# A bank for one values tile, smaller first pieces and fewer warm-up products in a hybrid decoder layer

## The chip, the cores and the metric

The kernel runs on one core of a Trainium2 chip. The metric is the device time of one execution in microseconds. The engines are named as in the profile: PE (TensorE's products) and PEld (its weight loads), DVE (VectorE), ACT (ScalarE), POOL (GpSimd) and SP (SyncE, which here issues DMAs).

## What is computed

One decoder layer on 512 tokens of width 1024, in float32. A normalized input is projected once; three groups of heads use the columns (dilated attention, gated linear attention "GLA", block-sparse attention); then come an output projection and a feed-forward part with a squared ReLU.

```python
h = rmsnorm(x, norm1_w)
proj = h @ w_in
aq, ak, av, bq, bk, bv, br, ba, cq, ck, cv = split(proj)
y_a = dilated_attention(aq, ak, av, bias_a)
y_b = gla(bq, bk, bv, br, ba, w_a2, b_a, gla_norm_w)   # ends with * silu(br)
y_c = moba_attention(cq, ck, cv, bias_c)
x = x + concat(y_a, y_b, y_c) @ w_out
x = x + square(relu(rmsnorm(x, norm2_w) @ w_ff1)) @ w_ff2
return rmsnorm(x, final_norm_w)
```

## The kernel before

**Products in three parts.** PE takes its operands in a rounded 32-bit form. To keep float32 accuracy every operand is cut in a high and a low part (`xh`, `xl` of the activations, `wh`, `wl` of the weights), and each product is made three times (high by high, low by high, high by low). The high part is a copy with a cast, on ACT or DVE; the low part is a subtraction on DVE.

**An order written out by hand.** The kernel's streams are Python generators. A planner (`Plan`, L111) runs them: it keeps a clock for each engine, gives each operation a cost of its own estimate, and places next the operation that can start first by those clocks, the lower priority number first among equals. What it places goes to its engine's queue in that order; the hardware then runs each queue in order, and semaphores that follow from the data hold an instruction until its inputs are there and its output's place is free. Streams also wait for events (`("wait", ...)`, set by `fire`) and for resources (`("take", r)`, given back by `give(r)`); both act on the planner's order. The PSUM banks are such resources: two of kind "mm", two "s", two "pt", one "o" and one "g" (L219).

**The start.** `start` (L1759) issues the DMA of the first weight block `wraw` on ACT's queue, sets `ones`, and gives PE a number of products of `ones` with itself (`WARM`, L28), whose result nobody reads; each shows as two passes in the profile. `first_x` brings the first block of the transposed input in two DMAs into `x0n`: 256 tokens and the norm weights (272 columns), then the other 256. `norm_weights` (L1746) copies 16 columns of norm weights to `nw` on DVE. `scaled_x(0)` makes `xh` of the first block by two activations of 256 columns on ACT, and later `xl` on DVE and squares on ACT. `parts` (L310) makes `wh` of the first weight block by one cast of 528 columns on DVE after `nw`; for all later blocks it uses ACT. `zeros` has POOL clear several tiles, the six `klz` halves among them.

**The first product.** `first` (L673) goes over eight blocks of 128 input columns. For each block and each of the three parts it makes four products of 272 weight columns (`av`, one per tile of 128 tokens) and two of 512 tokens (`bq`, `bk`), into six banks of kinds "s", "o", "g" and "pt".

**The first values product.** `v_proj(0)` (L1091) then makes, for each of the four token tiles, 24 products of 512 columns (`vps`: eight blocks, three parts, a group of three at a time) into a bank of kind "mm". `v_out` (L1073) empties the bank by two activations on ACT, `v` and `rg`, and gives it back. Meanwhile the GLA streams make small products that also take "mm" banks (`dps`, then the transposes `ktp`), and batches of level products (`lp`) into "s" and "pt" banks, which DVE empties by predicated copies into `attn`. `bias_table` (L622) uses "g" for the first half of a table and "o" for the second (`vt`, copied by DVE to `vals`). After `v_proj(0)` come the query and key products (`qkps`), whose weights `parts` cuts with ACT (`wh`) and DVE (`wl`). Almost every instruction carries line 141 in the profile, that of the helper that issues them, so the tiles' names tell them apart.

Of the kernel before, what the change touches and what calls it, by code (L numbers as in the profile page):

```python
# [12 lines left out]
AF = mybir.ActivationFunctionType  # L13
# [11 lines left out]
KBS = ((2,), (1, 3), (0,))  # L25
KO = (0, 1, 3, 4, 2, 5, 6, 7)
TAU = 1.0 / 16.0
LC, LT, LW, LN, WARM = 1.0, 0.5, 1.0, 0.0, 9  # L28
BIGS, SLOTS, WPAIRS, SCRATCH = 43, 22, 5, 2048
NC = 5  # L30
ZL, PL = 4.5, 3.2
# [76 lines left out]
PE, ACT, DVE, POOL, SP = (Engine(n) for n in ("tensor", "scalar", "vector", "gpsimd", "sync"))  # L108


class Plan:  # L111
# [15 lines left out]
    def spawn(self, gen, prio=0):  # L127
        self.streams.append(dict(gen=gen, prio=prio, item=None, at=self.now, sent=None, n=len(self.streams)))

    def fire(self, key, t=None):  # L130
        self.done[key] = self.now if t is None else t

    def give(self, res):
        self.free[res].append(self.now)
# [75 lines left out]
def hybrid_block_kernel(ctx: ExitStack, tc: tile.TileContext, x0_d, xT_d, x_d, w0_d, wv_d, wqk_d, w1_d, w2_d,  # L210
# [10 lines left out]
    spawn, fire, give = plan.spawn, plan.fire, plan.give  # L221
    late = dict(copy=LC, tt=LT)

    def slot(name, dt=F32, shape=(128, 512)):
        return sp.tile(list(shape), dt, name=name, tag="slot", bufs=SLOTS)

    def big(name, dt=F32, shape=(128, 1024)):
        return wp.tile(list(shape), dt, name=name, tag="big", bufs=BIGS)
# [4 lines left out]
    def bank(tag, name):  # L233
        return ps.tile([128, 512], F32, name=name, tag=tag, bufs=BANKS[tag])

    def f32(ap):
        return ap.bitcast(F32)
# [10 lines left out]
    nw = consts.tile([128, 2, KT], F32)  # L248
# [30 lines left out]
    xh, xl = ([t[:, k] for t in [big(n, F32R, (128, 2, 512)) for _ in range(4)] for k in range(2)] for n in ("xh", "xl"))  # L279
# [30 lines left out]
    def parts(key, src, n=1024):  # L310

        yield ("take", "w")
        yield ("take", "big")
        yield ("take", "big")
        hi = big("wh", F32R)
        lo = big("wl", F32R)
        loaded[key] = (hi, lo)
        if key == ("0", 0):
            yield ("wait", "nw")
        yield (DVE.tensor_copy(hi[:, :n], src[:, :n]) if key == ("0", 0) else ACT.activation(hi[:, :n], src[:, :n], AF.Copy))  # L320
        fire(("wh", key))
        if key == ("0", 0):
            yield ("wait", ("xl", 0))
        yield DVE.tensor_tensor(lo[:, :n], src[:, :n], f32(hi[:, :n]), op=OP.subtract)
        fire(("w", key))

    def give_w():
        give("w")
        give("big")
        give("big")  # L330
# [193 lines left out]
    def scaled_x(k):  # L524
        if k == 0:

            halves = (slice(0, 256), x0n[:, :256]), (slice(256, 512), x0n[:, 272:528])
            n_ = x0n[:, 256:257]
            for i, (cs, src) in enumerate(halves):
                yield ("wait", ("x", 0, i))  # L530
                yield ACT.activation(xh[0][:, cs], src, AF.Copy, scale=n_)
                fire(("xh", 0) if i else "xh00")
            yield ("wait", ("wh", ("0", 0)))
            for cs, src in halves:
                yield DVE.scalar_tensor_tensor(xl[0][:, cs], src, n_, f32(xh[0][:, cs]), op0=OP.mult, op1=OP.subtract)
            fire(("xl", 0))
            for cs, src in halves:
                yield ACT.activation(ssx[:, cs], src, AF.Square)
            fire(("ssx", 0))
            give("big")  # L540
            return
        yield ("wait", ("x", k))
        yield ("wait", "nw")
        yield ACT.activation(xh[k], xT[k], AF.Copy, scale=nw[:, 0, k:k + 1])
        fire(("xh", k))
        if k == 1:
            yield ("wait", ("w", ("0", 0)))
        yield DVE.scalar_tensor_tensor(xl[k], xT[k], nw[:, 0, k:k + 1], f32(xh[k]), op0=OP.mult, op1=OP.subtract)
        fire(("xl", k))
        sq = slot("sq")  # L550
        yield ("wait", ("ssx", k - 1))
        yield ACT.activation(sq, xT[k], AF.Square)
        yield DVE.tensor_tensor(ssx, ssx, sq, op=OP.add)
        fire(("ssx", k))
# [118 lines left out]
    def first():  # L673

        for k in range(KT):
            yield ("wait", ("xh", k) if k else "xh00")
            yield ("wait", ("wh", ("0", k)))
            wh, wl = loaded.pop(("0", k))
            for i, (xx, ww) in enumerate(((xh[k], wh), (xl[k], wh), (xh[k], wl))):
                if i:  # L680
                    yield ("wait", (("xl", k), ("w", ("0", k)))[i - 1])
                kw = dict(start=(k == 0 and i == 0), stop=(k == KT - 1 and i == 2))
                ops = ([PE.matmul(acc_v[t][:, :272], xx[:, t * 128:(t + 1) * 128], ww[:, :272], **kw) for t in range(NT)]
                       + [PE.matmul(acc_q, ww[:, 272:400], xx, **kw), PE.matmul(acc_k, ww[:, 400:528], xx, **kw)])
                if k + i == 0:
                    yield ops[:2]
                    yield ("wait", ("xh", 0))
                    ops = ops[2:]
                yield ops
            give_w()  # L690
            if k == 5:
                fire("first6")
        fire("first")
# [376 lines left out]
                             stop=(last and i == len(ks) - 1 and j == 2))  # L1070
                   for j, (ww, xx) in enumerate(((wh, ah[k]), (wh, al[k]), (wl, ah[k])))]

    def v_out(g, t, acc):  # L1073

        n = 512 if g else 256
        v = vS[g, t] = vT[(g, t - t % 2) if g else (0, 0)][:, t % (2 if g else 4)]
        yield ACT.activation(v, acc[:, :n], AF.Copy, scale=rstd[:, t:t + 1])
        fire(("v", g, t))
        if not g:
            sg, rg = (x[:, t % 2] for x in gates[t // 2])  # L1080
            yield ACT.activation(rg, acc[:, n:], AF.Copy, scale=nrstd[:, t:t + 1])
        give("mm")
        if g:
            return
        yield ("prio", 2)
        yield [DVE.tensor_scalar(sg, rg, 80.0, None, op0=OP.min), DVE.tensor_tensor(rg, rg, gw, op=OP.mult)]
        fire(("gate", t))
        if t % 2:
            spawn(gate(t // 2), 2)

    def v_proj(g):  # L1091
        if not gates:
            gates.extend(tuple(slot(x, shape=(128, 2, 256)) for x in ("sg", "rg")) for _ in range(2))
        hl = []
        for c in range(4):
            yield ("wait", ("w", ("v", g, c)))
            hl.append(loaded.pop(("v", g, c)))
        for t in range(NT):
            yield ("take", "mm")
            acc = bank("mm", "vps")  # L1100
            ts = slice(t * 128, (t + 1) * 128)
            for k in range(KT):
                wh, wl = hl[k // 2]
                w_ = slice((k % 2) * 512, (k % 2) * 512 + 512)
                yield [PE.matmul(acc, xx[:, ts], ww[:, w_], start=(k + j == 0), stop=(k == 7 and j == 2))
                       for j, (xx, ww) in enumerate(((xh[k], wh), (xl[k], wh), (xh[k], wl)))]
                if t == NT - 1 and k % 2:
                    give_w()
                if t == NT - 1 and g and k % 2:
                    give("big")  # L1110
                    give("big")
                    if k > 4:
                        give("w")
            if t == 0:
                yield ("wait", "rstd")
                yield ("wait", "consts")
            if t % (2 if g else 4) == 0:
                yield ("take", "big")
                vT[g, t] = big("v", shape=(128, 2, 512) if g else (128, 4, 256))
                if t:  # L1120
                    fire("vT")
            spawn(v_out(g, t, acc), 0.5)

    def q_out(p, acc):
        yield ("wait", "R")
# [52 lines left out]
    def gate(i):  # L1178


        for t in (2 * i, 2 * i + 1):
            yield ("wait", ("gate", t))
        sg, rg = gates[i]
        y, d = (slot(x, shape=(128, 2, 256)) for x in ("y", "d"))
        yield ACT.activation(sg, sg, AF.Exp)
        yield ACT.activation(y, sg, AF.Ln, bias=1.0)
        yield ACT.activation(y, y, AF.Exp, scale=-1.0)
        yield [DVE.scalar_tensor_tensor(d, sg, 1.0, y, op0=OP.add, op1=OP.mult),
               DVE.scalar_tensor_tensor(d, d, -2.0, y, op0=OP.add, op1=OP.mult),
               DVE.tensor_tensor(rg, d, rg, op=OP.mult)]  # L1190
        G.append(rg.rearrange("p t c -> p (t c)"))
        if i:
            fire("G")
# [550 lines left out]
            fire(("x", 0, i))  # L1744

    def norm_weights():  # L1746
        yield ("wait", ("x", 0, 0))
        yield DVE.tensor_copy(nw.rearrange("p a b -> p (a b)"), x0n[:, 256:272])
        fire("nw")

# [133 lines left out]
```

## Time and profile before

| | us |
|---|---|
| median of three runs | 556.94 |
| lowest, highest | 556.84, 557.59 |
| the profiled execution | 556.4 |
| its span, first to last instruction | 554.6 |

Times of instructions are from the span's start. In the lines of the timeline the columns are start, duration, engine, line, operation, out<-in tiles, shape and count, and in brackets the idle time of the engine before it with what ended it. A matmul's end is modelled; the distance from one start to the next says more than its duration. In the tables by engine, (x) is the number of instructions. DMA was busiest at the start; the page's two rows on it in 40 slices of the span are:

```profile
DMA  8930304699998969803679714688815788937504
GB/s 314 392 136 2 110 6 132 215 281 253 273 285 275 316 201 376 171 1 115 152 157 281 212 72 153 152 221 234 228 38 190 160 223 230 212 79 209 106 1 152
```

### The profile page before, as it was taken

What the parts mean: (1) busy time and instruction counts of PE and PEld (TensorE: products, weight loads), DVE (VectorE), ACT (ScalarE), POOL (GpSimd) and SP (SyncE); (2) the same over time, 40 slices, a digit from 0 to 9 for tenths busy, and PEclk for the clock granted to TensorE, in tenths of its full rate; (3) what the DMA queues carried; (4) which work ended last, traced back from release to release, by engine and by line L of the source; (5) the groups of instructions that cost most, each with busy time, mean ns of one, the idle gap of its engine ahead of it and who ended that gap; (6) DMA issues with size and microseconds to landing.
All of it is one profiled execution on the core that took longest, in us unless ns stands there. A gap on an engine that the chain in (4) does not pass through costs nothing.

```text
span 554.6 us, 9438 instructions
## 1 busy us (share of the span) xinstructions
PE 546.1 (98%) x3530; PEld 484.8 (87%) x3530; DVE 488.0 (88%) x793; ACT 351.2 (63%) x588; POOL 84.6 (15%) x135
## 2 busy tenths in 40 slices
PE   9999999999999999999999999999999999999995
PEld 8987888888888888999988999988999888999884
DVE  6969998999987899899899858999589999588986
ACT  7746465668576546768855448864377753479654
POOL 7100000431524001100111100111000111202031
PEclk9999999999999999999999999999999999999998
DMA  8930304699998969803679714688815788937504
GB/s 314 392 136 2 110 6 132 215 281 253 273 285 275 316 201 376 171 1 115 152 157 281 212 72 153 152 221 234 228 38 190 160 223 230 212 79 209 106 1 152
DMA packets 33518, 101.44 MB, mean 183 GB/s; under 512 B 5026, under 2 KB 5712, under 8 KB 33472
## 3 DMA queue, kind: packets, MB, share of 16 engines
q1 hardware_dynamic: 24816, 73.76, 39.3%
q0 software_dynamic: 8368, 26.53, 24.5%
q8 instruction: 28, 0.46, 0.3%
q10 hardware_dynamic: 288, 0.53, 0.3%
q14 instruction: 18, 0.15, 0.1%
HBM read 92.11 MB, written 8.71 MB: 182 GB/s over the span
## 4 chain that ended last, share of the span: by engine, by line
PE 98%; DVE 1%; issue 0%; ACT 0%; DVEq 0%
PE f2X L141 19%; PE f1V L141 15%; PE qkps L141 12%; PE f2W L141 10%; PE vps L141 8%; PE f1W L141 7%; PE f2Y L141 5%; PE f L141 4%; PE f1X L141 4%; PE sps L141 3%; PE po L141 2%; PE av L141 2%; PE lp L141 1%; PE bk L141 1%; PE bq L141 1%; PE op L141 1%
## 5 line engine op out<-in xcount | busy, mean ns | idle before, releaser
L141 POOL DMA_DIRECT2D w2raw<-in_w x36 | 31.7, 907 | 301.9 <-DVE wl L141 199.1
L141 DVE TENSOR_TENSOR wl<-w2raw,wh 128x1024 fp32r<-128x1024 f32 x56 | 68.4, 1238 | 2.6 <-ACT wh L141 2.6
L141 ACT ACTIVATE wh<-w2raw 128x1024 fp32r<-128x1024 f32 x56 | 58.2, 1050 | 17.3 <-PE f2Y L141 12.5
L141 PE MATMUL f2X<-wh,Ah 128*128 128x512 f32 (+1 forms) x160 | 62.3, 390 | 0.0
L141 PE MATMUL f2X<-wh,Al 128*128 128x512 f32 (+1 forms) x160 | 61.9, 387 | 0.0
L141 PE MATMUL f2X<-wl,Ah 128*128 128x512 f32 (+1 forms) x160 | 61.9, 387 | 0.0
L141 ACT ACTIVATE wh<-w1raw 128x1024 fp32r<-128x1024 f32 x42 | 43.3, 1051 | 29.2 <-DVE w1raw L141 27.6
L141 DVE TENSOR_TENSOR wl<-w1raw,wh 128x1024 fp32r<-128x1024 f32 x42 | 50.8, 1222 | 12.3 <-ACT wh L141 12.3
L141 PE MATMUL f1V<-Uh,wl 128*128 128x256 f32 x168 | 47.6, 283 | 0.0
L141 PE MATMUL f1V<-Ul,wh 128*128 128x256 f32 x168 | 47.6, 283 | 0.0
L141 PE MATMUL f1V<-Uh,wh 128*128 128x256 f32 x168 | 47.6, 283 | 0.0
L141 ACT ACTIVATE h<-h 128x512 f32<-128x512 f32 x53 | 33.3, 629 | 17.8 <-DVE h L141 17.1
L141 PE MATMUL qkps<-xh,wh 128*128 128x512 f32 x96 | 38.1, 397 | 0.0
L141 PE MATMUL qkps<-xh,wl 128*128 128x512 f32 x96 | 37.5, 390 | 0.0
L141 PE MATMUL qkps<-xl,wh 128*128 128x512 f32 x96 | 37.5, 390 | 0.0
L141 ACT ACTIVATE P<-P,mn 128x512 f32<-128x512 f32 (+3 forms) x48 | 26.6, 556 | 15.6 <-DVE mn L141 15.4
L141 PEld LDWEIGHTS f2X<-wh,Ah 128*128 128x128 f32 x160 | 30.1, 188 | 6.9 <-issue 1.0
L141 DVE TENSOR_TENSOR wl<-wraw,wh 128x1024 fp32r<-128x1024 f32 (+1 forms) x32 | 34.5, 1087 | 1.5 <-ACT wh L141 1.4
L141 PEld LDWEIGHTS f2X<-wl,Ah 128*128 128x128 f32 x160 | 30.1, 188 | 6.1
L141 PEld LDWEIGHTS f2X<-wh,Al 128*128 128x128 f32 x160 | 30.1, 188 | 5.8
L141 ACT ACTIVATE Ah<-s 128x512 fp32r<-128x512 f32 x40 | 23.8, 623 | 15.8 <-DVE s L141 15.3
L141 PEld LDWEIGHTS f1V<-Uh,wh 128*128 128x128 f32 x168 | 32.3, 192 | 0.0
(297 smaller groups left out, 1675.7 us busy)
## 6 DMA issues: line engine op xcount, KB each, us to landing
w2raw<-in_w SPq DMA_DIRECT2D x42, 512.0 KB
w2raw<-in_w POOLq DMA_DIRECT2D x36, 512.0 KB, 7.0
w1raw<-in_w SPq DMA_DIRECT2D x28, 512.0 KB
wraw<-in_wqk SPq DMA_DIRECT2D x12, 512.0 KB
turn<-tb SPq DMA_DIRECT2D x10, 512.0 KB
thb<-turn POOLq DMA_DIRECT2D x40, 128.0 KB, 5.9
wraw<-in_wv SPq DMA_DIRECT2D x8, 512.0 KB
woraw<-in_w SPq DMA_DIRECT2D x8, 512.0 KB
```

Source lines behind the costliest of these rows:

```text
L141: getattr(getattr(self.nc, op.eng), op.method)(*op.args, **op.kw)
```

## The change

- `WARM` is 7 instead of 9.
- The first `wh` is cast in two pieces, 272 and 256 columns, and no longer waits for `nw`; the copy to `nw` is placed after both.
- The first half of the first `xh` is made in two activations of 128 tokens; the second half stays one activation of 256.
- The first three products are placed one by one, each after the piece that it reads; the rest of the group follows once all of `wh` is there.
- In `v_proj(0)` the third token tile takes the bank of kind "o" instead of "mm", and `v_out` gives that one back.

```diff
-LC, LT, LW, LN, WARM = 1.0, 0.5, 1.0, 0.0, 9
+LC, LT, LW, LN, WARM = 1.0, 0.5, 1.0, 0.0, 7
...
         if key == ("0", 0):
-            yield ("wait", "nw")
-        yield (DVE.tensor_copy(hi[:, :n], src[:, :n]) if key == ("0", 0) else ACT.activation(hi[:, :n], src[:, :n], AF.Copy))
+            yield DVE.tensor_copy(hi[:, :272], src[:, :272])
+            fire("wh00")
+            yield DVE.tensor_copy(hi[:, 272:n], src[:, 272:n])
+        else:
+            yield ACT.activation(hi[:, :n], src[:, :n], AF.Copy)
         fire(("wh", key))
...
                 yield ("wait", ("x", 0, i))
-                yield ACT.activation(xh[0][:, cs], src, AF.Copy, scale=n_)
-                fire(("xh", 0) if i else "xh00")
+                for part in (slice(0, 256),) if i else (slice(0, 128), slice(128, 256)):
+                    yield ACT.activation(xh[0][:, cs][:, part], src[:, part], AF.Copy, scale=n_)
+                    fire(("xh", 0) if i else "xh00" if part.start else "xh000")
...
-            yield ("wait", ("xh", k) if k else "xh00")
-            yield ("wait", ("wh", ("0", k)))
+            yield ("wait", ("xh", k) if k else "xh000")
+            yield ("wait", ("wh", ("0", k)) if k else "wh00")
...
                 if k + i == 0:
-                    yield ops[:2]
-                    yield ("wait", ("xh", 0))
-                    ops = ops[2:]
+                    for op, event in zip(ops, ("xh00", ("xh", 0), ("wh", ("0", 0)))):
+                        yield op
+                        yield ("wait", event)
+                    ops = ops[3:]
                 yield ops
...
-    def v_out(g, t, acc):
+    def v_out(g, t, acc, r):
...
-        give("mm")
+        give(r)
...
-            yield ("take", "mm")
-            acc = bank("mm", "vps")
+            r = "o" if (g, t) == (0, 2) else "mm"
+            yield ("take", r)
+            acc = bank(r, "vps")
...
-            spawn(v_out(g, t, acc), 0.5)
+            spawn(v_out(g, t, acc, r), 0.5)
...
     def norm_weights():
-        yield ("wait", ("x", 0, 0))
+        yield ("wait", ("wh", ("0", 0)))
         yield DVE.tensor_copy(nw.rearrange("p a b -> p (a b)"), x0n[:, 256:272])
```

## The prediction

> **What bounds the kernel now.** I read the page's table of engines and its chain first, then the list of PE's waits.
>
> ```profile
> span 554.6 us, 9438 instructions
> PE 546.1 (98%) x3530; PEld 484.8 (87%) x3530; DVE 488.0 (88%) x793; ACT 351.2 (63%) x588; POOL 84.6 (15%) x135
> PE 98%; DVE 1%; issue 0%; ACT 0%; DVEq 0%
> PE warm L141 <- DVE eps L141: 1.1, 1, 1.1
> PE vps L141 <- ACT rg L141: 0.6, 1, 0.6
> ```
>
> TensorE's products are the chain. In the whole span its list has two waits: 1.1 us before the first warm-up, which the change leaves, and 0.6 us in the values product. So little can be won: that wait, some tenths at the start, and what the shift does later. DVE, 88% busy, is the engine that can take a gain back. About 0.2% (1.1 us) is what a measurement of this kernel can tell from no change.
>
> **Third tile, step by step.** The timeline around the wait, PE, then its weight loads, then ACT:
>
> ```profile
> 49.77 0.40 PE L141 MATMUL vps<-wl,xh 128*128 128x512 f32 x1
> 50.01 0.49 PE L141 MATMUL ktp<-cst,ek 128*128 128x128 f32 x3
> 51.09 0.51 PE L141 MATMUL vps<-wh,xh 128*128 128x512 f32 x1 [0.60 <-ACT rg L141]
> 51.44 0.40 PE L141 MATMUL vps<-wh,xl 128*128 128x512 f32 x1
> 51.09 0.19 PEld L141 LDWEIGHTS vps<-wh,xh 128*128 128x128 f32 x1 [0.84 <-ACT rg L141]
> 49.28 0.16 ACT L141 ACTIVATE dg<-dps 128x16 f32<-128x16 f32 x1
> 50.20 0.47 ACT L141 ACTIVATE v<-vps,rstd 128x256 f32<-128x256 f32 x1 [0.76 <-PE vps L141]
> 50.58 0.47 ACT L141 ACTIVATE rg<-vps,nrstd 128x256 f32<-128x256 f32 x1
> ```
>
> Two "mm" banks exist. At 50.01 the transposes ktp hold one and the third tile the other, so the fourth tile waits until rg has emptied it (50.58 + 0.47 = 51.05). The three ktp passes, 0.107 apart, are through at 50.33: PE stands for 51.09 - 50.33 = 0.76. With the third tile in "o", the fourth takes the bank that dg emptied at 49.28 + 0.16 = 49.44, long before. A product behind a wait also runs up slower: 51.09 to 51.44 is 0.35 where 0.23 is the pace; some 0.03 more comes from there. **Gain 0.79.**
>
> Is "o" free? The users that come next are the second half of the bias table (vt) and, far later, the state updates.
>
> ```profile
> 41.32 0.39 PE L141 MATMUL vps<-wh,xh 128*128 128x512 f32 x1
> 41.99 0.31 PE L141 MATMUL vt<-oneh,rb 128*128 128x320 f32 x1
> 41.71 0.47 DVE L141 COPY vals<-vt 12x320 f32<-12x320 f32 x1
> 81.90 0.47 DVE L141 COPY vals<-vt 12x320 f32<-12x320 f32 x1
> ```
>
> The third tile asks for its bank when the second's last group is placed, ahead of 41.32; the second vt only after the copy of the first. So the tile gets "o" and vt goes behind its eviction, near 51: its 0.15 us of PE moves and costs nothing new, and its copy at 81.90 is thirty microseconds away. If vt came first, main would wait for a copy that DVE makes at 81.90; that would be tens of microseconds, but this order speaks against it.
>
> What is late next? The level products (lp) and DVE:
>
> ```profile
> 54.76 2.01 PE L141 MATMUL lp<-kq 32*128 32x64 f32 x64
> 53.58 0.45 DVE L141 COPY_PREDICATED attn<-lmask,lp 128x256 f32<-128x256 int32 x1
> 60.30 0.44 DVE L141 COPY_PREDICATED attn<-lmask,lp 128x256 f32<-128x256 int32 x1
> 62.37 2.01 PE L141 MATMUL lp<-kq 32*128 32x64 f32 x64
> 64.40 2.64 DVE L141 COPY_PREDICATED attn<-lmask,lp 128x256 f32<-128x256 int32 x6 [1.22 <-PE lp L141]
> 70.67 1.22 DVE L141 TENSOR_TENSOR wl<-wraw,wh 128x1024 fp32r<-128x1024 f32 x1
> 72.15 0.19 PEld L141 LDWEIGHTS qkps<-xh,wl 128*128 128x128 f32 x1
> 72.38 0.39 PE L141 MATMUL qkps<-xh,wl 128*128 128x512 f32 x1
> ```
>
> The lp batches need banks that DVE's predicated copies empty at 54.03 and 60.74; DVE does not move with PE there. A lead of 0.79 is about one group of three products (0.68), so I take it that the planner puts one more group ahead of a batch: the third batch then starts at 62.37 - 0.79 + 0.68 = 62.26, only 0.11 earlier. DVE, idle 1.22 until that batch, moves by 0.11, and the wl of the next weights ends at 70.67 + 1.22 - 0.11 = 71.78 instead of 71.89. PE with its lead wants to load it at 72.15 - 0.79 = 71.36, so it waits, loads at 71.82 (0.04 for the signal, as 51.05 to 51.09) and multiplies about 0.12 later, 71.94 instead of 72.38. **The lead left is 0.44**; 0.35 is lost to DVE. Bounds: 0.79 if the batch keeps its place in PE's order (DVE then moves as well), 0 if other steps of DVE slip too. I take 0.44 because these rows give it. After this the wait list has nothing, so what is left reaches the end.
>
> **Start.** Warm-ups, casts and POOL's memsets before:
>
> ```profile
> 1.06 4.02 PE L141 MATMUL warm<-ones 128*128 128x128 f32 x18 [1.06 <-DVE eps L141]
> 4.80 0.56 PEld L141 LDWEIGHTS av<-wh,xh 128*128 128x128 f32 x4
> 5.42 0.40 PE L141 MATMUL bq<-xh,wh 128*128 128x512 f32 x1
> 3.92 0.46 DVE L141 COPY nw<-x0n 128x16 f32<-128x16 f32 x1 [2.91 <-DMA x0n<-in_x]
> 4.12 0.54 DVE L141 CAST wh<-wraw 128x528 fp32r<-128x528 f32 x1
> 3.83 0.52 POOL L141 MEMSET klz<- 64x512 f32 x1
> 4.41 0.71 POOL L141 MEMSET klz<- 64x512 f32 x1
> 3.92 0.51 ACT L141 ACTIVATE xh<-x0n 128x256 fp32r<-128x256 f32 x1 [1.45 <-DMA x0n<-in_x]
> 4.48 0.51 ACT L141 ACTIVATE xh<-x0n 128x256 fp32r<-128x256 f32 x1
> 5.20 0.72 ACT L141 ACTIVATE xh<-xT,nw 128x512 fp32r<-128x512 f32 x1 [0.21 <-DMA xT<-in_xT]
> L141 ACT ACTIVATE ssx<-x0n 128x256 f32<-128x256 f32 x2 | 0.7, 401 | 0.0
> L141 ACT ACTIVATE sq<-xT 128x512 f32<-128x512 f32 x7 | 4.2, 617 | 0.0
> ```
>
> Warm-ups: 18 passes, (4.02 - 0.40) / 17 = 0.213 apart; 14 of them end near 5.08 - 4 x 0.213 = 4.23 instead of 5.08. They now hold back the first real product: wh is ready at 4.12 + 0.54 = 4.66, the load starts at 4.80, with the last pass.
>
> Casts: nw (16 columns in 0.46) ends at 4.38, just after the memset that ends at 4.35, and the memset at 4.41 takes 0.71 where its fellows take 0.52: copies and memsets exclude each other. The cast ran from 4.38 to 4.66, 0.28 for 528 columns. The first piece, 272 columns, thus also starts at 4.36 and takes 0.14: 4.52 (at least 4.26, at 4.12 + 0.14, if it needn't wait; at most 4.66). [...]
>
> Activations: 401 against 617 makes 0.216 for 256 columns; 128 columns take 0.51 - 0.11 = 0.40, the next piece following 0.09 earlier than that. Three pieces start at 3.92, 4.23 and 4.54 and the last ends at 4.54 + 0.51 = 5.05 instead of 4.99. PE's first two products can load at 4.56 (wh at 4.52 + 0.04), but the third needs this last piece: 5.09, where before its load began at 5.04. The run-up then gives a product at 5.20; before, counting 0.127 per product back from bq's 5.42, it was at 5.17. So splitting moves the first products, not the stream: 0.03 later, **cost 0.03**, bounds -0.24 (all moves with the first load, 4.80 to 4.56) and +0.1. I round the start to nothing.
>
> nw now comes behind the casts. xh of the second block (5.20) needs it, with an idle of 0.21 as cover, and xl of the first block stands behind it on DVE; PE asks for that one product after bq, near 5.42 + 0.24 = 5.66, which leaves half a microsecond. No DMA is moved; SP's queue is untouched.
>
> **Sum.** -0.79 + 0.35 + 0 = -0.44. The profiled execution took 556.4 (span 554.6 and 1.8 around it), so 556.0 for its like; the median of the runs shown is 556.94, hence **556.5**.
>
> **Rivals.**
> 1. *The whole lead survives* (lp keeps its place): -0.79, 556.15. For it: DVE's idle of 1.22 at 64.40 shows room. Against: a group just fits.
> 2. *A memset gets in between the two casts and again before nw.* Memset 4.52 to 4.98, second piece to 5.14, memset to 5.60, nw to 5.63, xl in 0.42 more at 6.05: PE, which wants it near 5.69, is 0.4 late, and the second xl adds 0.1. Start +0.5, total +0.06: 557.0. For it: the memset of 4.41 was already asking.
> 3. *The clock gate sees the new gap* (the slower end). Rows:
>
> ```profile
> L141 PEld LDWEIGHTS warm<-ones x18: 250/333/333, 1.1 to 4.6; 128*128 128x128 f32 x18
> L141 PEld LDWEIGHTS av<-wh,xh x4: 188/190/192, 4.8 to 5.2; 128*128 128x128 f32 x4
> 550.90:554.60 3.70, 0.00 (x0) 0.00 (x0) 0.00 (x0) 0.00 (x0) 0.00 (x0) 0.50 0.45 157
> ```
>
> Loads took 333 ns in the warm-ups and 190 from 4.80 on: PE ran slow for 3.7 us from 1.06 and fast after unbroken work; after the end the granted clock is 0.50. With seven warm-ups PE idles from 4.2 to 4.56 and before the third product. If that breaks the count and it starts again at 5.20, PE runs at half speed until 8.9: 1.85 lost, total +1.41, 558.35. It decides as soon as the gap counts as idle. [...] Against: some 0.7 of 3.7 us is idle, four fifths still busy.
> 4. *"o" isn't had without a wait*, the stall only changes its name: 556.9.
> 5. *More than the sum*: the start moves by 0.24 and the lead survives, with a stall or two of DVE's going as the planner reorders: -1.2, 555.75.
>
> **How the numbers follow.** Forecast 0.36, rival 1 0.20, rival 2 0.15, rival 3 0.11, rival 4 0.06, rival 5 0.12. Range 555.6 to 557.6: it leaves out rival 3 and the far end of rival 5. Faster by over 0.2% (below 555.8): rival 5 and the better third of rival 1, 0.18. Slower (above 558.05): rival 3 and 0.01 of the rest, 0.12. Within: 0.70.
>
> **What would show it.** Right: no wait of vps for rg; the second vt behind the third tile, near 51; six qkps groups before the third lp batch; a short wait of qkps for DVE's wl near 71.8; PE's stream after the third product as before within 0.1. Wrong: lp batch near 61.6 (rival 1); a klz memset between the casts (2); loads of 333 ns among the av products beyond 5.5 (3); PE waiting in front of the third tile (4). I would be wrong outright if the planner's new order opened a stall far behind, where nothing of before warns of it.

## The result, and the profile after

The change makes the kernel **slower by 1.4%**: 564.86 us (median of five, 563.48 to 567.09) against 557.49 for the kernel before beside it, ratio 1.0143 with a 95% interval of 1.0126 to 1.016. The forecast was 556.5, with a range up to 557.6; none of its rivals reaches this time. The profiled execution took 563.48 with a span of 561.7, that is 7.1 more than the span of before.

The chain that ended last, by engine, was PE 98% before. After the change:

```profile
PE 82%; DMA 8%; DVE 7%; issue 2%; ACT 1%; DVEq 0%; SPq 0%; POOLq 0%; ACTq 0%
```

PE's waits after the change (total, times, longest). The wait of `vps` for `rg` is gone; four others are there that the kernel before did not have:

```profile
PE po L141 <- ACT v L141: 2.7, 1, 2.7
...
PE sps L141 <- DVE mn L141: 1.0, 1, 1.0
PE av L141 <- DVE wh L141: 0.3, 1, 0.3
PE f2W L141 <- DVE x L141: 0.2, 1, 0.2
```

**Where the time goes.** I compare, product by product, the distance to the next product with the usual one for its kind, and add up what is above it. After 66 us the changed kernel is even with the one before (in these two traces its start is 0.5 later, with 0.27 more at 11.4; the third tile gave 0.76 back). It then falls behind by 1.5 near 148, by 4.9 from 181 to 200 and by 0.5 at 207; with small pieces that is the 7.1. All of it lies between 146 and 208, some 95 us and more behind the third tile.

The stages by windows (length, then busy time of PE, PEld, DVE, ACT, POOL, then the clock, DMA share and GB/s); first the kernel before, then the changed one:

```profile
150.00:181.00 31.00, 31.00 (x168) 25.98 (x168) 26.10 (x63) 22.26 (x52) 10.85 (x20) 1.00 0.95 277
181.00:201.00 20.00, 20.00 (x176) 16.20 (x172) 17.89 (x25) 9.80 (x13) 0.00 (x0) 1.00 0.82 258
```

```profile
150.00:181.00 31.00, 31.00 (x161) 25.82 (x161) 19.75 (x69) 20.30 (x57) 8.74 (x16) 1.00 0.88 263
181.00:201.00 20.00, 17.26 (x162) 13.70 (x161) 20.00 (x23) 8.35 (x11) 4.35 (x8) 0.91 0.94 276
```

Read the third pair of numbers, DVE: from 150 to 181 it is busy for 19.75 us instead of 26.10, so 6.3 us of work are pushed on, and from 181 to 201 it has no gap left (20.00 of 20.00) while PE has some. It did not begin there: DVE had already done 1.6 us less from 66 to 118 (48.29 instead of 49.89) and 1.4 less from 118 to 150 (29.56 instead of 30.95), though PE's one wait in that time is the 1.0 for `mn`. So PE waits mostly not in the stage in which DVE loses the time, but in the one behind it. DMA is nearly full in this stretch too (0.95 of its engines' time before); its row of 40 slices has four nines in a row from 111 to 166 us, so the start is not its one busy stretch.

The steps of that, from the timelines of SP's queue, DVE, ACT and PE of the changed kernel:

```profile
155.13 0.43 SPq L141 DMA_DIRECT2D turn<-t2s  x1
...
158.70 0.32 SPq L141 DMA_DIRECT2D turn<-tb  x1
159.12 4.80 SPq L141 DMA_DIRECT2D woraw<-in_w  x6
164.02 6.21 SPq L141 DMA_DIRECT2D zt<-rzt  x4
```

```profile
180.52 0.21 DVE L141 STREAM_TRANSPOSE rzt<-rz 128x32 f32<-128x32 f32 x1 [8.89 <-DMA zt<-rzt]
181.75 2.35 DVE L141 TENSOR_TENSOR t<-woraw 128x1024 f32<-128x1024 f32 x2
```

```profile
180.97 1.06 ACT L141 ACTIVATE wh<-woraw 128x1024 fp32r<-128x1024 f32 x1 [4.31 <-DMA turn<-tb]
183.06 2.19 ACT L141 ACTIVATE wh<-t 128x1024 fp32r<-128x1024 f32 x2 [1.03 <-DVE t L141]
185.16 0.67 ACT L141 ACTIVATE v<-vps,rstd 128x512 f32<-128x512 f32 x1
```

```profile
182.33 0.88 PE L141 MATMUL po<-thb,v 128*64 128x128 f32 x12
185.88 1.39 PE L141 MATMUL po<-thb,v 128*64 128x128 f32 x20 [2.68 <-ACT v L141]
```

And the same steps of the kernel before:

```profile
146.01 0.43 SPq L141 DMA_DIRECT2D turn<-t2s  x1
146.94 1.68 SPq L141 DMA_DIRECT2D zt<-rzt  x4
148.85 0.83 SPq L141 DMA_DIRECT2D woraw<-in_w  x2
153.96 3.90 SPq L141 DMA_DIRECT2D woraw<-in_w  x4
```

```profile
168.50 1.23 DVE L141 TENSOR_TENSOR t<-woraw 128x1024 f32<-128x1024 f32 x1 [0.29 <-DMA woraw<-in_w]
```

```profile
179.56 0.69 ACT L141 ACTIVATE v<-vps,rstd 128x512 f32<-128x512 f32 x1 [1.91 <-PE vps L141]
```

The last `turn` transfer of the fourth pair of heads (`t2s`, for which `woraw` waits in the code) leaves at 155.13 instead of 146.01, 9.1 us later; the fifth pair's first one (158.70) now stands ahead of `woraw` too, and `woraw` starts at 159.12 instead of 148.85, all six in one go. The four `zt` of the fourth pair, ahead of `woraw` before (146.94), are now behind it, and the last of them leaves near 170 (164.02 + 6.21). DVE's `rzt` of the sixth pair writes over what these `zt` read, so DVE stands still for 8.89; `t<-woraw` comes 13.2 us later than before; ACT's casts of `t` wait for it, and `v` stands behind these casts. So 2.68 us of PE at 183 are paid for something that began before 150.

### The profile page after: what moved, and what is told of

The parts are those of the page before. It is cut to its first block, busy times and chain, and to the rows that moved or that the text cites. A ratio compares the mean times of both kernels' runs of the same rounds, so it can differ in the third digit from the quotient of the medians.

```text
span 561.7 us, 9431 instructions
## 1 busy us (share of the span) xinstructions
PE 549.5 (98%) x3526; PEld 485.7 (86%) x3526; DVE 488.2 (87%) x794; ACT 350.8 (62%) x589; POOL 84.7 (15%) x135
## 4 chain that ended last, share of the span: by engine, by line
PE 82%; DMA 8%; DVE 7%; issue 2%; ACT 1%; DVEq 0%; SPq 0%; POOLq 0%; ACTq 0%
PE f2X L141 18%; PE f1V L141 14%; PE f2W L141 9%; PE qkps L141 8%; PE f1W L141 7%; PE f2Y L141 5%; PE f L141 4%; PE vps L141 4%; PE f1X L141 4%; DMA woraw<-in_w 3%; PE av L141 2%; DMA wraw<-in_wv 2%; DMA turn<-tb 2%; PE sps L141 1%; PE lp L141 1%
```

## The experiments

To tell the change from what the planner makes of it, some runs keep an order that was written down. In these the planner's choice of the next step (the earliest start by its clocks) is replaced by the place of the step in a list, for all engines; a step whose resource is not free yet is passed over until it is. Nothing else changes:

```diff
-                    if cand is None or (t, st["prio"], st["n"]) < cand[:3]:
-                        cand = (t, st["prio"], st["n"], st, o)
+                    if cand is None or (rank, st["prio"], st["n"]) < cand[:3]:
+                        cand = (rank, st["prio"], st["n"], st, o, t)
```

"The old order" is the list of the kernel before; "the new order" that which the planner writes once the third tile takes the bank of kind "o". The start edits alone leave SP's order, and PE's but for the four missing warm-up passes, as they were; from 20 us on the whole change has the order of e1 on every engine.

| run | ratio to before | 95% interval | span of its profile |
|---|---|---|---|
| e1 tile alone | 1.0173 | 1.0152 to 1.0194 | 564.2 |
| e2 start alone | 1.0012 | 1.0003 to 1.0022 | 557.1 |
| e3 tile, old order | 1.0001 | 0.9992 to 1.001 | 554.8 |
| e4 no edit, new order | 1.0152 | 1.0135 to 1.0169 | 561.8 |
| e5 tile, old order, vt behind | 0.9988 | 0.9979 to 0.9997 | 556.0 |
| e6 tile, new order to 80 us, then old | 0.9991 | 0.9981 to 1.0 | 554.0 |
| e12 whole change, old order, vt behind | 0.9994 | 0.9984 to 1.0004 | 553.8 |
| e10 start with nine warm-ups | 1.0 | 0.9991 to 1.0009 | 555.4 |
| e11 seven warm-ups alone | 1.0004 | 0.9996 to 1.0013 | 555.5 |
| e16 tile, new order to 105 us, then old | 1.0027 | 1.0017 to 1.0036 | 556.2 |
| e7 tile, new order to 118 us, then old | 1.0031 | 1.0019 to 1.0043 | 558.2 |
| e17 tile, old order to 133 us, then new | 1.0196 | 1.0179 to 1.0213 | 567.4 |
| e8 no edit, old order, two DMAs late | 1.014 | 1.0126 to 1.0154 | 562.8 |
| e9 new order, these steps early | 1.015 | 1.0122 to 1.0178 | 566.3 |
| e13 new order, woraw behind zt | 1.0153 | 1.0101 to 1.0205 | 563.2 |
| e14 new order, v ahead of the casts | 1.0155 | 1.0135 to 1.0175 | 564.6 |
| e15 both | 1.0124 | 1.0074 to 1.0174 | 561.2 |
| e18 tile, cuts first | 1.0131 | 1.0116 to 1.0146 | 563.4 |

### Edit or order: e1 to e4

Theory A: the order costs the time. B: the start and the warm-ups do. C: the bank itself does.

e1 takes only the bank from the change:

```diff
-            yield ("take", "mm")
-            acc = bank("mm", "vps")
+            r = "o" if (g, t) == (0, 2) else "mm"
+            yield ("take", r)
+            acc = bank(r, "vps")
```

> Of the change only the bank of the third tile, with the planner free; nine warm-ups and the start as before. The planner then writes PE's order of the changed kernel. Theory A (the new order costs the time: 7.07 us between the spans, of which about 0.5 to 0.8 is the start): slower by about 6.4, ratio 1.011 to 1.012. Theory B (the start and the missing warm-ups cost it, by way of the clock or a late stream): faster by 0.4 to 0.8, ratio 0.999. Theory C (the bank of kind o itself costs it, by what must wait for that bank): as A, 1.011 to 1.013.

e2 takes all the rest (casts, activations, `nw`, `first`, `WARM = 7`):

> Of the change all but the bank: seven warm-ups, two casts, three activations, nw behind the casts. The planner then writes PE's order of the kernel before. A: slower by 0.5 to 0.8, as late as the stream was in the changed kernel after the start, ratio 1.001. B: slower by 6 to 7, ratio 1.011 to 1.013. C: as A.

e3 is e1 with the old order:

> The third tile in the bank of kind o, start as before, but every engine's order is that of the kernel before (written down and followed), save for the second vt, which has to come behind the third tile. A: the wait of 0.76 for rg goes and nothing else moves: faster by 0.4 to 0.8, ratio 0.9987. C: slower by about 6, ratio 1.011.

e4 is the kernel before with the new order, every bank and every piece as before:

> No edit of the change at all: banks, casts and warm-ups as before, but every engine follows the order that the planner wrote for the third tile in the bank of kind o. A: slower by 6 to 8 (the wait for rg is back and the order is the bad one), ratio 1.011 to 1.014. C and B: no difference beyond half a microsecond, ratio 0.999 to 1.001.

Measured: 1.0173, 1.0012, 1.0001, 1.0152. e4 settles it: **without any edit, the new order alone costs 8 us**. B falls by e2, C by e3. e1 is slower than A and C had it; its profile has two stretches of low clock more than those of e4 and of the whole change (mean granted clock 0.988 against 0.994 and 0.995; see the end). e3 also missed its own number, since I expected 0.9987. Its timeline of PE says why:

```profile
50.97 0.42 PE L152 MATMUL vt<-oneh,rb 128*128 128x320 f32 x1 [0.60 <-ACT rg L152]
51.22 0.39 PE L152 MATMUL vps<-wh,xh 128*128 128x512 f32 x1
```

The fourth tile no longer waits, but `vt`, which needs the same bank "o" from the same `rg`, stood right in front of it: the wait had only changed its name.

### What the direct parts are worth: e5, e6, e12

In e5 `vt` goes behind two groups of the fourth tile, in the old order:

```diff
 ktp
-vt (second half)
 vps, fourth tile: two groups of three
+vt (second half)
```

> As the run with the third tile in the bank of kind o and the order of the kernel before, but with the second vt behind the second group of three products of the fourth tile instead of ahead of its first. Theory: in the run before this one the wait of 0.77 for rg was not gone, it stood at vt instead of vps. With vt behind 1.36 us of products nothing waits for rg, so PE gains the whole 0.76 at 51 and, since every other place in the order is kept, keeps it: ratio 0.9986. Rival (the step of the prediction that gives 0.35 back to DVE's wl near 71.8): 0.9993. Rival (DVE or ACT eats all of it in the attention): 1.000.

e6 follows the new order up to the first half of the query and key products, then the old one:

> Third tile in the bank of kind o, start as before; the new order up to the first half of the query and key products (near 80 us), from there the order of the kernel before. If the loss is opened behind 80 us: the gain at 51 less 0.35 for wl, ratio 0.9986 to 0.9995. If the six groups ahead of the third lp batch or the later up open it: slower by 3 or more, ratio 1.005 and up.

e12 is the whole change, start included, in the old order with `vt` behind two groups:

> The whole change (bank, casts, activations, seven warm-ups), in the order of the kernel before, with the second vt behind the second group of the fourth tile: the direct parts of the change without the planner's answer. Theory: the gain of 0.6 to 0.7 by the bank and the loss of 0.6 by the start cancel, ratio 0.999 to 1.001. If bank or start also have a cost that only shows together: 1.002 and up.

0.9988, 0.9991 and 0.9994. PE's wait list has no `rg` in e5 and only the warm-up's in e6, whose span is 554.0 against 554.6 although its stream began 0.15 later: **0.77 gained at 51 and kept to the end**. e5 is faster than the kernel before by 0.1%; e6 by nearly as much, with an interval that just reaches 1. e12 cannot be told from no change. (That e5's profile spans 556.0 is a start 0.7 late and a stretch at low clock near 50, told at the end; it was the longest of its eleven executions.)

### The start: e2, e10, e11

e10 is e2 with `WARM = 9`; e11 is the kernel before with `WARM = 7`.

> The start as changed (two casts, three activations, nw behind them), but nine warm-ups; banks and order as before. If it is the two missing warm-ups that make the start late (PE idle ahead of the first product, the TensorE clock then rising later in some executions): ratio 0.999 to 1.000. If it is the two casts, between which a memset of POOL gets in: as late as with seven, ratio 1.001.

> The kernel before with seven warm-ups and nothing else. If the missing warm-ups make the start late: PE idle for 0.6 ahead of the first product, the clock rising later in some executions, ratio 1.001 to 1.002. If the casts do: 1.000.

1.0012, 1.0 and 1.0004. Only casts and missing warm-ups together differ from no change; the three intervals overlap, so how the 0.65 us divides stays open. PE in the changed kernel, then before (0.50 earlier), then in e12, which has the whole start of the changed kernel:

```profile
6.16 0.39 PE L141 MATMUL bk<-xh,wh 128*128 128x512 f32 x1
```

```profile
5.66 0.39 PE L141 MATMUL bk<-xh,wh 128*128 128x512 f32 x1
```

```profile
5.65 0.40 PE L152 MATMUL bk<-xh,wh 128*128 128x512 f32 x1
```

So the new start by itself need not be late. What differs is when PE gets fast: the weight loads of `bq` and `bk` take 330 ns at 5.56 and 5.79 in the changed kernel, but 189 and 188 at 5.30 and 5.42 in e12. That varies with the start untouched as well: this `bk` stands at 5.66 in the profile of e15, at 6.40 in e7 (its load takes 330 ns at 5.97) and at 6.83 in e14. One trace against one other says nothing of the change here.

The changed kernel's DVE and POOL, with the two casts apart:

```profile
4.24 0.30 DVE L141 CAST wh<-wraw 128x272 fp32r<-128x272 f32 x1 [3.23 <-DMA wraw<-in_w]
4.46 0.69 DVE L141 CAST wh<-wraw 128x256 fp32r<-128x256 f32 x1
5.07 0.57 DVE L141 COPY nw<-x0n 128x16 f32<-128x16 f32 x1
```

```profile
4.41 0.59 POOL L141 MEMSET klz<- 64x512 f32 x1
5.05 0.55 POOL L141 MEMSET klz<- 64x512 f32 x1
```

The second cast takes 0.69 for 256 columns where the first takes 0.30 for 272: the memset of 4.41 runs to 5.00 and the cast ends at 5.15, so I read it as having its turn behind the memset; beside the next memset (5.05 to 5.60) `nw` takes 0.57. (The two casts take 0.91 together here and 1.05 in e12, and there `bk` is not late.) In the profile of e2 PE's products stay slow for longer than in those of the changed kernel, e10, e11 and e12 (loads of 190 ns by 7.21 at the latest): 0.63 for a product of 512 columns at 6.27, 0.39 only at 9.71, where the kernel before has 0.40 at 5.42.

```profile
6.27 0.63 PE L141 MATMUL bq<-xh,wh 128*128 128x512 f32 x1
...
9.71 0.39 PE L141 MATMUL bq<-xh,wl 128*128 128x512 f32 x1
```

That execution took 558.88, the longest of e2's ten (the shortest 556.57).

### Where the new order loses: e7, e8, e9

In the new order two DMAs that bring weights of the second values product stand behind the third pair's `turn` in SP's queue. The reason in the code: `parts` gives a raw buffer back only when `wl` is placed, the planner's clock lets one `wl` slide behind softmax and transposes, and so `fetch` gets the buffer later. e7 changes back to the old order ahead of that point; e8 puts just these two DMAs late in the old order:

```diff
-wraw<-in_wv, third and fourth
 turn<-tb, turn<-t2s of the third pair
+wraw<-in_wv, third and fourth
```

> The same bank and start; the new order up to the scores of the third pair of heads (near 118 us), from there the order of the kernel before. Theory D (the loss starts where two weight DMAs of the second values product are placed behind turn in SP's queue, which lies behind this point): within 1 us, ratio 0.998 to 1.002. Theory E (no single place, the loss grows with the length of the new order): a good third of it, ratio 1.004 to 1.007.

> The kernel before, its banks, its start and its order, but two weight DMAs of the second values product are placed where the new order has them in SP's queue, behind the turn transfers of the third pair; the casts that need them wait for them and all else keeps its place. D: the casts come 8 to 12 us later, sit in front of other work on ACT and DVE, and PE waits: slower by 3 to 7, ratio 1.005 to 1.012. E: within 1 us, ratio 1.000 to 1.002.

1.0031 and 1.014: nearer to D than to E, but e7 keeps 1.7 us where D allows 1, and e8 costs more than D's range. e8's rows show the whole path of one transfer, from SP's queue to PE:

```profile
131.03 2.74 SPq L152 DMA_DIRECT2D turn<-tb  x2
134.34 1.42 SPq L152 DMA_DIRECT2D wraw<-in_wv  x2
```

```profile
139.80 1.06 ACT L152 ACTIVATE wh<-wraw 128x1024 fp32r<-128x1024 f32 x1 [5.93 <-DMA wraw<-in_wv]
```

```profile
140.89 1.22 DVE L152 TENSOR_TENSOR wl<-wraw,wh 128x1024 fp32r<-128x1024 f32 x1 [5.59 <-ACT wh L152]
```

```profile
143.80 0.48 PE L152 MATMUL sps<-k,q 128*128 128x128 f32 x1 [4.55 <-DVE mn L152]
```

SP issues from 134.34 on what the kernel before issued at 114.64 and 122.38; ACT's cast, and DVE's `wl` behind it, hold up softmax (`mn`), which does not need these weights at all but stands behind them; the scores (`sps`) wait for its bank, and from 142.6 to 149.4 the granted clock is 0.50. PE multiplies with these weights only from 158.1 on (its first `vps` of the second product).

So a late DMA is **enough** for such a loss. e9 asks whether it is the one that the new order pays for. It moves the two `wl`, one `wh` and both DMAs forward in the new order:

> Third tile in the bank of kind o, start as before, the whole new order, but five steps of it moved forward: the two wl subtractions (with the second one's wh cast) that free the raw buffers, and behind them the two weight DMAs that take these buffers, stand about 85 and 55 places earlier, close to where the order of the kernel before has them. Theory D (the late wl holds the raw buffer, the DMA then goes behind turn in SP's queue, and all of the loss follows from that): within 1.5 us of the kernel before, ratio 0.998 to 1.003. Theory E (other steps of the new order cost as much by themselves): slower by 4 or more, ratio 1.007 to 1.012.

1.015: **D falls**. The waits are other ones (`f2W` for `x` 2.8, `po` for `v` 2.2, `sps` for `mn` 1.8), their sum is not smaller.

### Taking the late waits away: e13, e14, e15

e13 puts the six `woraw` behind the four `zt` in SP's queue; e14 puts the last `v` ahead of the casts of `t` on ACT; e15 does both.

```diff
-woraw<-in_w x6
 zt<-rzt x4 (pair 3)
+woraw<-in_w x6
...
-wh<-t x2
 v<-vps
+wh<-t x2
```

> Third tile in the bank of kind o, start as before, the whole new order, but the six woraw DMAs stand behind the four zt DMAs of the fourth pair in SP's queue instead of ahead of them. Theory G (DVE's rzt waits 9.2 us for these zt, which wait in SP's queue behind woraw; DVE's next casts and ACT's come late by that, and v behind them on ACT): the wait of rzt falls under 2, the wait of po for v goes, and with it the stretch at half clock: 4 us of the 8 to 9 that the new order costs, ratio 1.006 to 1.009. Theory F (v only stands at the wrong place of ACT's queue, the casts ahead of it wait for turn anyway): no gain, ratio 1.014 to 1.018.

> The same new order, but on ACT the last v stands ahead of the two casts of t instead of behind them; in the run with the new order ACT sat idle for 1.48 ahead of these casts. F and G both: po then waits for v some 0.1 instead of 2.7, and 4 of the 8 to 9 us go if nothing else is late there, ratio 1.006 to 1.009. If po's next input (the moved scores by way of turn) is late as well, its wait only changes its name: 1.012 and up.

> Both of the edits of the two runs before. If they take away the same wait: as the better of them, 1.006 to 1.009. What is left is then the wait of sps near 148 (1.5 to 2) and what follows from it.

1.0153, 1.0155, 1.0124: each edit takes its own wait away, and the 4 us that G and F gave it do not come back (e15's four executions spread from 561.12 to 565.51, so a part may). In e13 `rzt` waits 0.4, and `v` is no longer what `po` waits for; in e14 `po` waits 0.6 for `v`. But PE's waits then read, e13 first, e14 second:

```profile
PE sps L152 <- DVE mn L152: 2.5, 1, 2.5
PE f2W L152 <- DVE x L152: 2.1, 1, 2.1
PE po L152 <- DMA th<-turn: 1.2, 1, 1.2
```

```profile
PE po L152 <- DVE h L152: 2.5, 1, 2.5
PE sps L152 <- DVE mn L152: 1.9, 1, 1.9
PE f2W L152 <- DVE x L152: 1.7, 1, 1.7
PE po L152 <- ACT v L152: 0.6, 1, 0.6
```

In e13 `t<-woraw` starts at 180.71, waiting for its DMA, 3.4 earlier than in e1 (184.12), which is the same kernel without the edit, but still 12.2 later than before. The edit has a price of its own: `woraw` leaves at 166.19 instead of 161.90. So most of DVE's arrears stay, and the next thing that needs DVE pays. Neither G's nor F's wait carries the loss alone; these waits are where the debt is collected.

### Where the debt is made: e16, e17, e18

e16 changes back to the old order ahead of the sliding `wl`; e17 keeps the old order until all weights of the fourth pair are cut and takes the new one from there; e18 lets the planner choose, with one number changed:

```diff
-    spawn(cut(), 3)
+    spawn(cut(), 0.9)
```

> Third tile in the bank of kind o, start as before; the new order up to the scores of the second pair (near 105 us, ahead of the place where the new order lets the wl of the fourth pair's weights slide behind the third pair's softmax), from there the order of the kernel before. Theory I (that slide is where the loss is opened: the fourth pair's scores, with them woraw, and in the end po come some 10 us late): no loss, ratio 0.998 to 1.001, less than the 1.003 of the run that changes back at 118 us. Theory E (it grows with the length): 1.002 to 1.003.

> The same bank and start; the order of the kernel before (second vt behind two groups of the fourth tile) until all weights of the fourth pair are cut (near 133 us), from there the new order. I: no loss, ratio 0.998 to 1.002. E, or a second place of its own behind 133 us (the woraw DMAs, the order of the last v): 1.006 and up.

> The third tile in the bank of kind o, start as before, with an order of the planner's own in which the stream that cuts the weights has a lower number (0.9 instead of 3), so that among steps that can start at the same time wl and wh come ahead of softmax and transposes. I: the wl of the fourth pair no longer slides, most of the 8 us do not come up, ratio 0.998 to 1.004. E: the order is another again and can cost as much, 1.005 and up.

1.0027, 1.0196, 1.0131. e16 and e7 together: changing back at 80 costs nothing (e6), at 105 us 1.5 us, at 118 us 1.7 us; most of the 8 us is opened behind 118. (The waits of `sps` for `mn` that e16 and e7 have, at 111 to 113 and at 127 to 128, lie right behind the change of order, so a part of the 1.5 and 1.7 may belong to the seam.)

e17 finds a loss behind 133 as well: with the old order up to there, the new one still loses 11 us, and the fourth pair's last `turn<-tb` leaves at 159.65, later than anywhere else (145.65 before). Theory I falls with both. e18 brings it to 145.84, as before, and loses as much near 200, where `po` waits 2.1 for `th` and `f2W` 2.3 for `x`.

E, a loss that grows with the length of the new order, does not fit either, since e17 has less of the new order and pays more. So I have no single step to point at: each of the orders that the planner wrote, whether from the start or from 133 on, makes other links to DVE's work late, and PE pays 7 to 11 us.

**What stays open** is which of the steps behind 118 makes the delay of the fourth pair. One candidate can be read off: in the changed kernel DVE makes this pair's `klz` and `q` from 132.43 to 136.68, before from 116.48 to 122.65, and its first scores follow at 137.15 instead of 128.87. But e18 has them as late (130.84 to 133.68) with `turn` in time, and e17 has them early (116.85 to 123.02) with `turn` late, so it is neither needed nor enough.

## Why the prediction was wrong, by its own steps

- **The third tile, 0.79.** Right: 0.77 in e6. The second `vt` stands at 51.71 in the changed kernel, "near 51", behind the third tile. "o" was had without a wait (rival 4 is out). e3 shows the trap next to it.
- **Six groups ahead of the third `lp` batch, 0.35 lost to `wl`.** Six it is: the batch starts at 62.45 in e6, with PE 0.59 ahead, 62.37 - 0.59 + 0.68 = 62.46. But no `wl` is late near 72, the lead stays whole. The step that failed: I moved the batch and left DVE's steps behind it in their sequence. The planner, with the batch one group later, put the next `wl` ahead of the batch's copies (e6's DVE):

```profile
64.01 1.22 DVE L152 TENSOR_TENSOR wl<-wraw,wh 128x1024 fp32r<-128x1024 f32 x1
66.70 3.14 DVE L152 COPY_PREDICATED attn<-lmask,lp 128x256 f32<-128x256 int32 x6
```

- **"I round the start to nothing."** Not the step that made the result, and not settled to some tenths. In e12 the new start is not late at all (`bk` at 5.65 against 5.66); e2's ratio says +0.65 (0.2 to 1.2). Rival 2's memset did come between the casts in the changed kernel (0.69 for the second one; both together take 0.91, in e12 1.05 and in e2 1.30), but in e12 its price of 0.5 was not paid. In the changed kernel the memset of 4.41 began while the first cast ran (4.24 to 4.54) and ended at 5.00, ahead of the second cast, which ended at 5.15 (0.69 instead of 0.30).
- **The clock after the gap (rival 3).** Its sign is there: loads of 330 ns at 5.56 and 5.79 in the changed kernel, and products of 0.63 in e2's profile until 9.7. But e7 shows such loads too, with its start untouched, and what it cost the changed kernel is 0.5 and not 1.85, so it isn't the result. That the gap starts the slow 3.7 us anew, up to 8.9, was an estimate: in the changed kernel a load takes 190 ns again at 6.76, in e2 only at 9.71.
- **"-0.79 + 0.35 + 0 = -0.44."** For the direct parts the sum was nearly right: e12 has 0.9994, or -0.3, with an interval of 0.5 to each side. In part that is luck: the 0.35 was not lost, and by e2 the start took about as much instead.
- **"After this the wait list has nothing, so what is left reaches the end."** This is the step that failed. "No DMA is moved; SP's queue is untouched" was said of the start and holds for it (e2 has SP's old order); of the tile I never asked it, and there it fails. A wait list of the kernel before says where the order before waits. With one bank of another kind, and with 0.77 us to gain from it, the planner wrote another order, on ACT and DVE from 57 us and on SP from 95 us on. Up to 80 us it costs nothing (e6); behind that it has on SP the fourth pair's `zt` behind `woraw` instead of ahead of it, and on DVE 6 us of work later. That order alone, with no edit, costs 8 us (e4). I named that ("the planner's new order opened a stall far behind"), gave it no price and no chance, and so left 558.35 as the slowest end. The profile did hold a warning: DVE was busy for 88% of the span, and for nearly all of 118 to 150 (30.95 of 32.00 before), with softmax, cuts and transposes of several streams in one queue. On an engine that full, an order is a result, not a detail.

## What to carry to other kernels

Where the order of the program comes from a planner, an edit has two prices: what it does at its place, and what the planner writes behind it; hold the order fixed once (replay it) to see them apart. Before forecasting, look not only for PE's waits but for the engine with no slack in the stages that follow, since each step that is late there is paid by whoever comes next. A wait that goes is only gone if nothing else in the queue asks for the same resource first (`vt` in e3), and taking a late wait away shows little when the engine behind it is in arrears (e13, e14).

## What the runs showed of the hardware that was not expected

A wait of PE cost more than its length here. After the 2.68 at 183 the granted clock of the changed kernel fell, although PE worked for some of the window:

```profile
184.00:187.00 3.00, 1.11 (x20) 1.12 (x22) 3.00 (x4) 1.75 (x3) 1.84 (x4) 1.00 1.01 313
187.00:190.40 3.40, 3.40 (x36) 3.40 (x34) 3.40 (x4) 0.00 (x0) 0.00 (x0) 0.50 1.08 249
```

3.4 us at half speed add 1.7 to the 2.7 (an estimate from this row). The wait of 1.9 near 149 in e1 had the same sequel (clock 0.51 from 151 to 153), that of 1.6 near 128 in e7 had not (1.00 throughout). Nor does a longer wait always have it: e14's of 2.52 that ends at 196.49 left the clock alone.

```profile
194.70:198.10 3.40, 1.61 (x28) 1.62 (x30) 3.13 (x5) 0.02 (x1) 0.00 (x0) 1.00 1.05 274
198.10:201.50 3.40, 3.40 (x35) 2.40 (x31) 3.40 (x5) 3.40 (x5) 0.00 (x0) 1.00 1.07 305
```

By the clock records of its trace the low stretch of the changed kernel lasts 3.413 us (187.00 to 190.41). In this trace and that of before the clock falls at whole multiples of this length from the first record of the clock: at 53 and at 162 of them in the changed kernel (from 6.09 to 187.00 and, after the last product, to 559.05), at 160 before (from 4.75 to 550.89, also after the last product). It seems to matter how much of the stretch between two such marks is idle, which is my reading of five rows and no more. PE was busy for 1.11 of 3.40 us from 183.6 to 187.0 in the changed kernel and for 1.44 of 3.40 from 147.6 to 151.0 in e1, and the clock fell at the end of both; it was busy for 1.61 in e14 (above) and 1.78 in e7 (126.4 to 129.8), and it did not. One stretch does not fit: e9 has 1.41 from 184.2 to 187.6 and kept its clock. What share of idle time decides, if it is the share, these runs do not show; a wait of 2.7, and in e1 of 1.9, was enough, and PE was busy for about a third of the 3 us ahead of the fall (1.11 of 3.00). At the start, the clock column of the profile's windows is no witness: it shows 1.00 from 6 to 9 us while products of e2 take 0.63, against 0.39 from 9.71 on.

The clock also fell with no wait at all, in two profiles: in e1's from 48.6 to 52.0 and in e5's, each time behind a batch of `lp` products (`32*128 32x64` in their rows). PE was busy throughout; e5's row:

```profile
49.50:53.00 3.50, 3.50 (x12) 2.74 (x11) 3.50 (x11) 2.09 (x7) 0.00 (x0) 0.51 0.00 0
```

The same batch left the clock alone in the kernel before (1.00 from 49.50 to 53.00) and in e6 (mean clock of its profile 0.997, as before). e5's own eleven executions have mean clocks from 0.993 to 0.998, so which execution has such a stretch seems not to be settled by the program alone.
